# Moving the block for over-full experts from the middle of the expert layer to its end

## The chip, the cores and the metric

The kernel runs on one core of one Trainium2 chip. The metric is device time in microseconds (us), taken as the median of several executions. A profile of one further execution gives the trace from which all rows below are read. The engines are called PE (matrix multiply; PEld is its weight load), ACT (activations), DVE (vector), POOL and SP; SP does no arithmetic here and issues nearly all DMA transfers.

## The reference, cut to what matters

Two layers, each with a mixer and then a mixture of experts. A token goes to two of 32 experts; each expert is a gated pair of products and a third product. What the change touches is the second half of a layer:

```python
def hier_moe(u, w_grp, b_grp, w_rt, b_rt, w1, w3, w2):
    ...
    eid = (g_idx * EXP_PER_GROUP + e_idx).reshape(TK)      # T = 512 tokens, TOP_K = 2
    ...
    def expert_block(args):
        xr, e = args
        return (jax.nn.silu(xr @ w1[e]) * (xr @ w3[e])) @ w2[e]
    ...

for layer in range(2):
    ...
    h = h + gt1 * m
    u = rms_norm(h, norm2[layer]) * (1.0 + sc2) + sh2
    h = h + gt2 * hier_moe(u, ...)
return rms_norm(h, final_norm)
```

The sum over experts is added to h, so the order of the experts is free as far as the sum goes. What follows the layer (the next layer's norm, or the final norm) needs the sum of squares of each row of the finished h.

## The kernel before, in words

h stays in SBUF as four tiles of 128 tokens by 1024 (`self.h(t)`, the tile `w` in the trace). The expert layer (`moe`, L1387) first routes: `posm` holds each token's place within its expert, `wcat` its weight. The 32 experts are then taken in 16 pairs, with 64 slots (`CAP`) for each expert. For two pairs at a time, PE multiplies the normalised tokens `hhi`/`hlo` with a one-hot matrix `Dm` (L1427) and so gathers the inputs `XTm`. For each pair PE computes the two products with w1 and w3 (L1506), ACT and DVE form `gg`, PE transposes it (L1536) and multiplies with w2 (L1560), and POOL, ACT and DVE form `yh`/`yl`. The step that adds a pair's result to h (`add`, L1567: PE L1574, DVE L1583) is put off: it is handed on as `before` and runs inside the next pair's step, in two halves, so that PE has work while DVE and ACT make `gg` and `hT`. Near the start of each pair POOL writes the small tile `sel` (L1515).

The weights of a pair are 12 MB, 12 transfers of 1 MB. `need` (L1365) issues them in a fixed order into some 15 buffers; a transfer waits until PE has read the buffer's last content. So SP's queue is a long row of transfers, each of which waits for PE.

An expert can get more than 64 tokens. For these, `overflow` (L1679) is a loop on the device: each turn takes 128 further tokens of such an expert, gathers them, fetches that expert's weights again and adds to h. The number of turns `nblk` is computed by `blocks` (L1666) and loaded into a register by every engine (L1686); the loop starts at L1688. The loop stands between the eighth and the ninth pair. Ahead of it the eighth pair's `add` is run out, so nothing is handed on across it. With the inputs used here no expert has more than 64 tokens in either layer: `nblk` is zero, and no instruction of the loop's body stands in the trace. What every engine does there is load the register, branch past the body, and wait at the loop's end: SP until all transfers that it has issued have landed, each engine until all engines and all transfer queues have reached their counts.

In the last pair, ACT squares each piece of h right after its last addition (L1587), with the sum going to `hss`; the squares themselves are not needed and are written over `hhi`. After layer 0 `restart` (L1912) takes the square root (`h_rstd`, L387), scales h into `hn`, and PE transposes that (L532); after layer 1 `finish` (L1825) multiplies the lower half of h with `fn`, the final norm's weights, on POOL (L1832), scales it on ACT (L1835), makes the upper half on DVE (L1836), and SP and ACT send the four tiles out (L1837).

Between Silu and Sqrt the compiled program holds a table load on ACT, an instruction of its own. `warm` (L1548) is a Sqrt of one element in the last pair, whose only use is that this load happens early.

Of the kernel before, what the change touches and what calls it, by code (L numbers as in the profile page):

```python
# [7 lines left out]
F32 = mybir.dt.float32  # L8
# [3 lines left out]
AF = mybir.ActivationFunctionType  # L12
OP = mybir.AluOpType
# [4 lines left out]
P = 128  # L18
D = 1024
# [3 lines left out]
EPS = 1e-6  # L23
# [1 line left out]
DE = 512  # L25
CAP = 64
BIG = 4096
OVER = 8
NPOOL = 3
PRI = 80  # L30
PIN = 12
# [11 lines left out]
def spread(x, h):  # L43

    return [x[:, c + j:c + 256:2] for c in (512 * h, 512 * h + 256) for j in range(2)]


def row_bcast(ap, n, parts=P):
    return bass.AP(tensor=ap.tensor, offset=ap.offset, ap=[[0, parts], [1, n]])
# [41 lines left out]
class Build:  # L91
# [1295 lines left out]
    def moe(self, es):  # L1387
        tc, nc, a, M = self.tc, self.nc, self.a, self.M
        l = M.l
        pool = M.pool  # L1390
        A, B = self.mod[l, 4], self.mod[l, 3]
        total = self.n_ext + 8
        M.more = self.pool(es, "more%d" % l, 2, side="right")
        first = ExitStack()
        M.first = self.pool(first, "first%d" % l, 2, side="right")
        posm = pool.tile([P, NT, NE], F32, name="posm")
        wcat = pool.tile([P, NT, 2, NE], F32R, name="wcat")
        self.need(total + 2)
        gate = self.gate_rows(l, 5)
        self.warm(WARM)  # L1400
        self.dump("lg%d" % l, M.lg)
        blocks = self.route(M.rt, M.lg, posm, wcat)
        self.dump("posm%d" % l, posm)
        M.rt_es.close()
        wk = self.pool(es, "mw%d" % l, 2)

        def onehot(e0):

            Dm = wk.tile([P, NT, 4, CAP], F32R, name="Dm", tag="Dm", bufs=1)
            with tc.high_priority(0 if e0 else PRI):  # L1410
                for t in range(NT):
                    nc.vector.tensor_tensor(Dm[:, t], posm[:, t, e0:e0 + 4, None].to_broadcast([P, 4, CAP]),
                                            self.slot_row[:, None, :].to_broadcast([P, 4, CAP]), op=OP.is_equal)
            return Dm

        inputs = lambda: wk.tile([P, KD, 4 * CAP], F32, name="XTm", tag="XTm", bufs=1)

        def dispatch(e0, Dm, XT):

            if not e0:  # L1420
                M.low()
            def blocks(ks):
                for k in ks:
                    p = self.ps([P, 4 * CAP])
                    for t in range(NT):
                        for i, src in enumerate((M.hhi, M.hlo)):
                            nc.tensor.matmul(p, spread(src[:, t], k // 4)[k % 4], Dm[:, t].rearrange("p e s -> p (e s)"),  # L1427
                                             start=t + i == 0, stop=t == NT - 1 and i == 1)
                    if k % 2:
                        nc.scalar.activation(XT[:, k], p, AF.Identity, scale=A[:, k:k + 1], bias=B[:, k:k + 1])  # L1430
                    else:
                        nc.vector.tensor_scalar(XT[:, k], p, A[:, k:k + 1], B[:, k:k + 1], op0=OP.mult, op1=OP.add)
            return Dm, XT, blocks


        XT = inputs()
        cur = dispatch(0, onehot(0), XT)

        self.need(total + 4)
        blocks = blocks()  # L1440
        before = Dnew = None
        for pr in range(NE // 2):
            if pr == OVER:
                for hb in range(2):
                    before(hb)
                before = None
                self.overflow(l, wk, wy, *blocks, posm, wcat, A, B, gate)

            self.need(12 * (pr + 1) + (total - 1 if pr == OVER - 1 else total))
            Dm, XT, make = cur  # L1450
            q = pr % 2
            tiles = [M.tiles.pop(12 * pr + i) for i in range(12)]
            p13 = self.ps(), self.ps()
            last = pr == NE // 2 - 1
            X = XT[:, :, q * P:(q + 1) * P]
            if not pr:

                for ks in range(4), range(4, KD):
                    make(ks)
                    for j in range(2):  # L1460
                        self.expert_in(p13, X, tiles, j, ks)
            else:
                self.expert_in(p13, X, tiles, 0, range(KD))
                if last:
                    for i in range(2):
                        before(i)
                    before = None
                self.expert_in(p13, X, tiles, 1, range(KD))
            if not pr:
                first.close()  # L1470
                wy = self.pool(es, "my%d" % l, 1, side="right")
                posT = wy.tile([NE, T], F32R, name="posT")
                p = self.ps([NE, T])
                for t in range(NT):
                    nc.tensor.transpose(p[:, t * P:(t + 1) * P], posm[:, t], self.ident)
                nc.vector.tensor_copy(posT, p)

            new = q and not last

            def early():  # L1480
                nonlocal Dnew
                if new:
                    Dnew = onehot(2 * pr + 2)

            def late():
                nonlocal cur
                if new:
                    cur = dispatch(2 * pr + 2, Dnew, inputs())
                    cur[2](range(KD))
            if last and l:  # L1490

                M.fn = wk.tile([P, D], F32, name="fn", tag="XTm", bufs=1)
                nc.sync.dma_start(M.fn, row_bcast(self.a["final_norm"], D))
            before = self.expert_pair(l, pr, *p13, tiles,
                                      lambda t: Dm[:, t].rearrange("p e s -> p (e s)")[:, q * P:(q + 1) * P],
                                      wk, wy, posT, wcat, gate, before, early, late)
        for i in range(len(M.cols)):
            before(i)

    def expert_in(self, ps, X, tiles, j, ks):  # L1500

# [6 lines left out]
    def expert_pair(self, l, pr, p1, p3, tiles, Dp, wk, wy, posT, wcat, gate, before, early, late):  # L1508


        nc, a, M = self.nc, self.a, self.M
        pin = self.tc.keep_in_program_order
        ea, last = 2 * pr, pr == NE // 2 - 1
# [37 lines left out]
        for c in cols:  # L1551
            py = self.ps([P, c.stop - c.start])
            hb = c.start // DE
# [13 lines left out]
        def add(n):  # L1567
            s = cols[n]
            if not (pr or n):
                self.new_h()  # L1570
            for t in range(NT):
                p = self.ps([P, s.stop - s.start])
                for i, y in enumerate((yh, yl)):
                    mm = nc.tensor.matmul(p, dt[:, t * P:(t + 1) * P], y[:, s], start=i == 0, stop=i == 1)  # L1574
                    if not last:
                        pin(mm)
                h = self.h(t)[:, s]
                part = lambda x, o: nc.vector.scalar_tensor_tensor(h, x[:, t, s].bitcast(F32), M.sd[:, t:t + 1], o,
                                                                   op0=OP.mult, op1=OP.add)
                if not pr:  # L1580
                    part(M.hhi, p)
                else:
                    nc.vector.tensor_add(h, h, p)  # L1583
                    if t == pr - 1:
                        part(M.hlo, h)
                if last:
                    nc.scalar.activation(M.hhi[:, t, s], h, AF.Square, accum_out=self.hss[:, n, t:t + 1])  # L1587
            if last and n == 1:
                nc.vector.tensor_add(self.hss[:, 0], self.hss[:, 0], self.hss[:, 1])
                nc.vector.tensor_scalar(self.hss[:, 0], self.hss[:, 0], 1.0 / D, EPS, op0=OP.mult, op1=OP.add)  # L1590
# [88 lines left out]
    def overflow(self, l, wk, wy, nblk, ends, over, posm, wcat, A, B, gate):  # L1679

        tc, nc, a, M = self.tc, self.nc, self.a, self.M
# [6 lines left out]
        with tc.For_i(0, n, 1):  # L1688
# [81 lines left out]
            for s in hs:  # L1770
                y32 = wy.tile([P, DE], F32, name="oy", tag="y32")
                nc.vector.scalar_tensor_tensor(y32, py[s.start // 512], wsl, gate[:, s], op0=OP.mult, op1=OP.mult)
                nc.scalar.activation(yh[:, s], y32, AF.Copy)
                nc.vector.tensor_sub(yl[:, s], y32, yh[:, s].bitcast(F32))
                for t in range(NT):
                    p = self.ps()
                    for i, y in enumerate((yh, yl)):
                        nc.tensor.matmul(p, DT[:, t], y[:, s], start=i == 0, stop=i == 1)
                    nc.vector.tensor_add(self.h(t)[:, s], self.h(t)[:, s], p)
            nc.vector.tensor_scalar(it, it, 1.0, None, op0=OP.add)  # L1780


# [178 lines left out]
```

## Time and profile before

| | |
|---|---|
| time, median of 3 executions | 1754.81 us (1753.83 to 1755.5) |
| the profiled execution: time | 1752.5 us |
| the profiled execution: span from first to last instruction | 1750.8 us |
| granted PE clock, mean over the span (1 is 2.4 GHz, 0.5 is 1.2 GHz) | 0.973 |
| PE busy | 1653.0 us (94%) |
| DVE, ACT, POOL busy | 804.0, 514.8, 394.8 us |
| HBM read | 492.21 MB |

Busy times are sums over stages with different limits, so they bound nothing by themselves. A stage is read from the windows of that stage; a stall is read from the idle time that the profile puts before an instruction, with the one that ended it.

### The profile page before, as it was taken

How to read it: one execution, taken by the hardware profiler on the slowest of the kernel's cores; microseconds unless marked ns; L12 is line 12 of the kernel's file. 1: busy time of each engine (PE TensorE's matmuls, PEld its weight loads, DVE VectorE, ACT ScalarE, POOL GpSimd, SP SyncE). 2: the span in 40 equal slices, each digit the busy share in tenths (PEclk: the TensorE clock that was granted, in tenths of full speed). 3: DMA queues.
4: the chain of work that ended last, by engine and by line, in shares of the span. 5: the costliest groups of instructions: out<-in, count | busy, mean ns of one | idle time of the engine just before them, and what ended most of it. 6: DMA issues, size and time to landing. Idle time of an engine off the chain costs nothing. (4 is left out here: it accounts for less than half of the span.)

```text
span 1750.8 us, 23258 instructions
## 1 busy us (share of the span) xinstructions
PE 1653.0 (94%) x9036; PEld 992.8 (57%) x9036; DVE 804.0 (46%) x1793; ACT 514.8 (29%) x1025; POOL 394.8 (23%) x350
## 2 busy tenths in 40 slices
PE   6999999899999899998989989899899999899997
PEld 3666767544555445454667667678544555455453
DVE  3345653432424224235787787855433334224234
ACT  4745333310110111014636475364310110111013
POOL 2443532210101001002534343353210011001001
PEclk9999999999999999999989999999999999999998
DMA  8655655689999899995233432237699999899994
GB/s 299 222 187 174 219 179 204 258 344 379 413 412 412 346 410 414 412 411 165 65 126 123 134 108 93 77 112 274 237 368 380 414 411 413 345 410 413 412 411 144
DMA packets 156052, 495.90 MB, mean 283 GB/s; under 512 B 16216, under 2 KB 43156, under 8 KB 140576
## 3 DMA queue, kind: packets, MB, share of 16 engines
q1 hardware_dynamic: 155488, 493.23, 73.2%
q8 instruction: 74, 1.21, 0.3%
q10 hardware_dynamic: 448, 1.11, 0.2%
q14 instruction: 42, 0.34, 0.1%
HBM read 492.21 MB, written 2.10 MB: 282 GB/s over the span
## 5 line engine op out<-in xcount | busy, mean ns | idle before, releaser
L1506 PE MATMUL ps<-w,XTm 128*64 128x512 f32 x2048 | 450.8, 597 | 11.5 <-SPq L1688 10.9
L1506 PEld LDWEIGHTS ps<-w,XTm 128*64 128x64 f32 x2048 | 155.8, 138 | 289.5 <-issue 281.1
L397 POOL TENSOR_TENSOR wlo<-w,whi 128x512 fp32r<-128x512 f32 x136 | 180.6, 1332 | 278.7 <-ACT whi L396 257.3
L1560 PE MATMUL ps<-w,hT 128*64 128x512 f32 (+1 forms) x1056 | 232.3, 590 | 1.6 <-ACT hT L1538 1.6
L1529 DVE TENSOR_TENSOR gg<-gg,ps 128x512 f32<-128x512 f32 x32 | 22.0, 688 | 395.6 <-PE ps L1506 395.6
L403 PE MATMUL ps<-w,whi 128*128 128x512 f32 x384 | 164.4, 429 | 0.1
L404 PE MATMUL ps<-w,whi 128*128 128x512 f32 x384 | 155.9, 406 | 2.2 <-POOL w L527 1.5
L1560 PEld LDWEIGHTS ps<-w,hT 128*64 128x64 f32 x1056 | 80.3, 138 | 134.2 <-issue 120.2
L405 PE MATMUL ps<-w,wlo 128*128 128x512 f32 x384 | 155.2, 405 | 0.0
L1583 DVE TENSOR_TENSOR w<-w,ps 128x512 f32<-128x512 f32 (+1 forms) x248 | 149.4, 662 | 8.5 <-PE ps L1574 7.2
L1515 POOL CAST sel<-ident 32x128 fp32r<-32x128 f32 x32 | 9.0, 281 | 617.0 <-PE ps L1543 499.9
L1564 POOL TENSOR_TENSOR yl<-y,yh 128x512 fp32r<-128x512 f32 x60 | 76.6, 1276 | 242.7 <-ACT yh L1563 242.7
L396 ACT ACTIVATE whi<-w 128x512 fp32r<-128x512 f32 x136 | 84.5, 626 | 145.6 <-PE ps L404 77.6
L1427 PE MATMUL ps<-Dm,hhi 128*128 128x256 f32 x512 | 125.8, 288 | 0.1
L1563 ACT ACTIVATE yh<-y 128x512 fp32r<-128x512 f32 (+1 forms) x66 | 40.8, 618 | 287.3 <-DVE y L1562 286.7
L1427 PE MATMUL ps<-Dm,hlo 128*128 128x256 f32 x512 | 123.4, 283 | 0.0
L1562 DVE SCALAR_TENSOR_TENSOR y<-ps,wsl,gate 128x512 f32<-128x512 f32 (+1 forms) x66 | 48.5, 734 | 147.4 <-PE ps L1560 72.4
L1427 PEld LDWEIGHTS ps<-Dm,hhi 128*128 128x128 f32 x512 | 101.1, 198 | 13.7 <-issue 13.5
L1574 PE MATMUL ps<-yh,dt 128*128 128x512 f32 (+1 forms) x264 | 105.6, 405 | 0.0
L1538 ACT ACTIVATE hT<-ps 128x512 f32<-128x512 f32 x32 | 19.1, 598 | 281.8 <-PE ps L1536 263.5
L1427 PEld LDWEIGHTS ps<-Dm,hlo 128*128 128x128 f32 x512 | 101.2, 198 | 0.0
L1574 PE MATMUL ps<-yl,dt 128*128 128x512 f32 (+1 forms) x264 | 100.8, 387 | 0.2 <-DVE yl L1564 0.2
(519 smaller groups left out, 2423.3 us busy)
## 6 DMA issues: line engine op xcount, KB each, us to landing
w<-in_moe_w_dram SPq DMA_DIRECT2D x380, 1024.0 KB, 12.6
w<-in_w_ada_dram SPq DMA_DIRECT2D x40, 1024.0 KB, 5.5
w<-in_w_in_c_dram SPq DMA_DIRECT2D x16, 1024.0 KB, 6.1
w<-in_w_in_ab_dram SPq DMA_DIRECT2D x10, 1024.0 KB
wst<-in_w_ada_dram SPq DMA_DIRECT2D x8, 1024.0 KB, 12.3
w<-in_w_out_ab_dram SPq DMA_DIRECT2D x4, 1024.0 KB, 4.8
w<-in_moe_w_dram SPq DMA_DIRECT2D x8, 512.0 KB, 10.4
w<-in_w_out_c_dram SPq DMA_DIRECT2D x4, 1024.0 KB, 4.8
```

The lines of the kernel that those rows point to most:

```text
L396: nc.scalar.activation(hi, src, AF.Copy)
L397: nc.gpsimd.tensor_sub(lo, src, hi.bitcast(F32))
L403: mm(p, lhs[0], rhs[0], start=start, stop=False)
L404: mm(p, lhs[0], rhs[1], start=False, stop=False)
L405: mm(p, lhs[1], rhs[0], start=False, stop=stop)
L1427: nc.tensor.matmul(p, spread(src[:, t], k // 4)[k % 4], Dm[:, t].rearrange("p e s -> p (e s)"), start=t + i == 0, stop=t == NT - 1 and i == 1)
L1506: self.nc.tensor.matmul(ps[j][half[e]], X[:, k, half[e]], w, start=k == 0, stop=k == KD - 1)
L1560: nc.tensor.matmul(py[half[e]], hT[:, k, half[e]], w, start=k == 0, stop=k == 3)
L1562: nc.vector.scalar_tensor_tensor(y32, py, wsl, gate[:, c], op0=OP.mult, op1=OP.mult)
L1564: (nc.vector if last else nc.gpsimd).tensor_sub(yl[:, c], y32, yh[:, c].bitcast(F32))
L1574: mm = nc.tensor.matmul(p, dt[:, t * P:(t + 1) * P], y[:, s], start=i == 0, stop=i == 1)
L1583: nc.vector.tensor_add(h, h, p)
```

## The change

The call of `overflow` moves from ahead of the ninth pair to behind the last one, in both layers. Its code is the same but for two lines at its end, which the new place asks for: since h can still change there, each turn squares h again. As the loop's body still needs `hhi`, the last pair's squares go to a scratch area `M.squares` of 1024 columns, half of the tile `fn`, that all four token tiles share.

```diff
         for pr in range(NE // 2):
-            if pr == OVER:
-                for hb in range(2):
-                    before(hb)
-                before = None
-                self.overflow(l, wk, wy, *blocks, posm, wcat, A, B, gate)
-
-            self.need(12 * (pr + 1) + (total - 1 if pr == OVER - 1 else total))
+            self.need(12 * (pr + 1) + total)
...
-            if last and l:
-
-                M.fn = wk.tile([P, D], F32, name="fn", tag="XTm", bufs=1)
-                nc.sync.dma_start(M.fn, row_bcast(self.a["final_norm"], D))
+            if last:
+
+                fn = wk.tile([P, 2, D], F32, name="fn", tag="XTm", bufs=1)
+                M.fn, M.squares = fn[:, 0], fn[:, 1]
+                if l:
+                    nc.sync.dma_start(M.fn, row_bcast(self.a["final_norm"], D))
...
         for i in range(len(M.cols)):
             before(i)
+        self.overflow(l, wk, wy, *blocks, posm, wcat, A, B, gate)
...
-                    nc.scalar.activation(M.hhi[:, t, s], h, AF.Square, accum_out=self.hss[:, n, t:t + 1])
+                    nc.scalar.activation(M.squares[:, s], h, AF.Square, accum_out=self.hss[:, n, t:t + 1])
...
                     nc.vector.tensor_add(self.h(t)[:, s], self.h(t)[:, s], p)
+                    nc.scalar.activation(M.squares[:, s], self.h(t)[:, s], AF.Square,
+                                         accum_out=self.hss[:, 1 + s.start // 512, t:t + 1])
+            nc.vector.tensor_scalar(self.hss[:, 0], self.hss[:, 1], 1.0 / D, EPS, op0=OP.mult, op1=OP.add)
             nc.vector.tensor_scalar(it, it, 1.0, None, op0=OP.add)
```

On SP, in the expert layer of layer 0, the loop stood between the weight transfers of before (`nblk` is the register load at the loop's entry; the body begins with the load of `ei`):

```order
L132 DMA w<-in_moe_w_dram 128x2048 x4
L132 DMA w<-in_moe_w_dram 128x2x1024 x2
L1686 TENSOR_LOAD nblk
L1688 COMPARE_AND_BRANCH
L1688 UNCONDITIONAL_BRANCH x2
L1956 BRANCH_PREFETCH_HINT
L1733 TENSOR_LOAD ei
```

In the changed kernel SP reaches it behind all weight transfers of the layer and behind the first transfers of the next layer's mixer; here is its end, with what follows:

```order
L1249 DMA wr<-in_moe_w_grp_dram 128x2x4
L1682 TENSOR_LOAD nblk
...
L1684 REGISTER_ALU
L1684 COMPARE_AND_BRANCH
L1684 UNCONDITIONAL_BRANCH
L1249 DMA wr<-in_moe_w_grp_dram 128x2x4
L1249 DMA wr<-in_moe_w_rt_dram 128x2x32 x2
L1252 DMA br<-in_moe_b_grp_dram 128x4
L1253 DMA br<-in_moe_b_rt_dram 128x32
L134 DMA w<-in_w_ada_dram 128x4x512
```

So one transfer of 1 MB (`in_w_ada`) and five small ones, which were issued while the last pair ran, now follow the loop. On ACT, the end of layer 0 reads before as follows (the squares write `hhi`, `hr` is the square root, `whi` a rounded copy of the next mixer's weights):

```order
L1587 ACTIVATE hhi,hsq<-w 128x512
L1587 ACTIVATE hhi,hsq<-w 128x256 x6
L396 ACTIVATE whi<-w 128x512
L1587 ACTIVATE hhi,hsq<-w 128x256 x2
L387 ACTIVATE hr<-hsq 128x1 x3
L1919 ACTIVATE hn<-w,hr 128x512 x3
L387 ACTIVATE hr<-hsq 128x1
L396 ACTIVATE whi<-w 128x512
L1919 ACTIVATE hn<-w,hr 128x512
```

and in the changed kernel as follows:

```order
L1583 ACTIVATE fn,hsq<-w 128x256 x8
L1682 TENSOR_LOAD nblk
L1684 COMPARE_AND_BRANCH
...
L1684 UNCONDITIONAL_BRANCH
L386 ACT_TABLE_LOAD
L386 ACTIVATE hr<-hsq 128x1 x4
L1918 ACTIVATE hn<-w,hr 128x512 x4
L395 ACTIVATE whi<-w 128x512 x2
```

The loop now stands between the squares and the roots. Since its body holds a Silu, a table load stands behind it, whether or not the body runs. The first copies `whi` stand behind `hn`. On POOL, at the end of layer 1, the four products `out` stood right behind the last `yl` (which is written for the last pair but one), free to start as soon as h is final:

```order
L1564 TENSOR_TENSOR yl<-y_13258,yh 128x512
L1832 TENSOR_TENSOR out<-w,fn 128x512 x4
```

In the changed kernel the loop stands ahead of them, as it does on each engine; in layer 0 POOL's first steps for the next mixer are moved behind it in the same way:

```order
L1560 TENSOR_TENSOR yl<-y_13024,yh 128x512
L1682 TENSOR_LOAD nblk
L1684 COMPARE_AND_BRANCH
L1684 UNCONDITIONAL_BRANCH x2
L1955 BRANCH_PREFETCH_HINT
L1684 REGISTER_ALU
L1684 COMPARE_AND_BRANCH
L1684 UNCONDITIONAL_BRANCH
L1831 TENSOR_TENSOR out<-w,fn 128x512 x4
```

## Rows read from the trace of the kernel before

**Rows 1.** The page's first part: busy time and share, PE's line.

```profile
PE 1653.0 (94%) x9036; PEld 992.8 (57%) x9036; DVE 804.0 (46%) x1793; ACT 514.8 (29%) x1025; POOL 394.8 (23%) x350
```

**Rows 2.** Windows of layer 0: stretch, its length, busy per engine, clock, DMA share and GB/s.

```profile
core 0: us, PE busy (x) PEld busy (x) DVE busy (x) ACT busy (x) POOL busy (x), PEclk, DMA share, GB/s
499.00:559.00 60.00, 60.00 (x307) 31.76 (x306) 20.76 (x39) 7.18 (x12) 5.68 (x6) 1.00 1.02 413
...
578.00:583.00 5.00, 0.00 (x0) 0.00 (x0) 1.51 (x3) 0.00 (x0) 0.00 (x0) 0.77 0.58 229
583.00:587.00 4.00, 3.94 (x10) 1.24 (x12) 0.00 (x0) 0.00 (x0) 0.00 (x0) 0.50 0.59 200
...
818.00:824.50 6.50, 2.88 (x19) 2.39 (x18) 6.14 (x17) 5.69 (x25) 3.52 (x5) 0.89 0.00 1
```

**Rows 3.** Timeline of POOL: the tile `sel`, around the middle of either layer.

```profile
559.33 0.28 POOL L1515 CAST sel<-ident 32x128 fp32r<-32x128 f32 x1 [14.34 <-PE ps L1543]
...
627.71 0.28 POOL L1515 CAST sel<-ident 32x128 fp32r<-32x128 f32 x1 [16.18 <-PE ps L1543]
...
687.71 0.28 POOL L1515 CAST sel<-ident 32x128 fp32r<-32x128 f32 x1 [16.20 <-PE ps L1543]
...
1478.33 0.28 POOL L1515 CAST sel<-ident 32x128 fp32r<-32x128 f32 x1 [14.34 <-PE ps L1543]
...
1546.48 0.28 POOL L1515 CAST sel<-ident 32x128 fp32r<-32x128 f32 x1 [16.18 <-PE ps L1543]
```

**Rows 4.** Timeline of PE: after the loop (either layer), after layer 0, an `in_w_ada` reader.

```profile
583.06 1.97 PE L1506 MATMUL ps<-w,XTm 128*64 128x512 f32 x4 [5.28 <-SPq L1688]
...
826.24 3.82 PE L532 MATMUL ps<-ident,hn 128*128 128x128 f32 x16 [5.35 <-ACT hn L1919]
...
870.70 1.06 PE L259 MATMUL ps<-w,cond 128*32 128x512 f32 x8
...
1502.40 1.98 PE L1506 MATMUL ps<-w,XTm 128*64 128x512 f32 x4 [5.64 <-SPq L1688]
```

**Rows 5.** Sequencer events of L1688 by engine: duration min/median/max ns, first and last start.

```profile
L1688 SPq EVENT_SEMAPHORE  x17: 17/17/28, 567.4 to 583.1; - x17
...
L1688 DVEq EVENT_SEMAPHORE  x3: 21/50/50, 579.5 to 580.3; - x3
...
L1688 ACTq EVENT_SEMAPHORE  x8: 38/38/38, 1501.3 to 1501.9; - x8
```

**Rows 6.** Timeline of ACT at the end of layer 0.

```profile
808.74 1.28 ACT L1548 ACT_TABLE_LOAD   x1
810.03 0.20 ACT L1548 ACTIVATE warm<-one 128x1 f32<-128x1 f32 x1
...
820.10 0.40 ACT L1587 ACTIVATE hhi<-w 128x256 fp32r<-128x256 f32 x1
820.41 0.19 ACT L1587 ACTIVATION_READ_ACCUMULATOR hhi<-w 128x1 f32 x1
820.50 0.40 ACT L1587 ACTIVATE hhi<-w 128x256 fp32r<-128x256 f32 x1
...
823.81 0.65 ACT L387 ACTIVATE hr<-hsq 128x1 f32<-128x1 f32 x3
825.47 1.95 ACT L1919 ACTIVATE hn<-w,hr 128x512 f32<-128x512 f32 x3 [1.01 <-DVE hr L388]
```

**Rows 7.** Timeline of SP, the issues at the end of layer 0.

```profile
805.11 1.26 SPq L1250 DMA_DIRECT2D wr<-in_moe_w_grp_dram  x2
...
812.45 0.38 SPq L135 DMA_DIRECT2D w<-in_w_ada_dram  x1
```

**Rows 8.** Timelines of ACT, POOL and DVE at the end of layer 1.

```profile
1742.26 0.19 ACT L1587 ACTIVATION_READ_ACCUMULATOR hhi<-w 128x1 f32 x1
...
1745.82 0.36 ACTq L1837 DMA_DIRECT2D out_dram<-out  x1
...
1734.81 5.32 POOL L1832 TENSOR_TENSOR out<-w,fn 128x512 f32<-128x512 f32 x4 [22.46 <-DVE w L1583]
...
1742.28 0.75 DVE L1836 SCALAR_TENSOR_TENSOR out<-w,hr,fn 128x512 f32<-128x512 f32 x1
```

More of the change, by code (lines that the diff above doesn't have):

```diff
@@ L27 @@
 BIG = 4096
-OVER = 8
 NPOOL = 3
```

## The prediction

> **What bounds the kernel now.** I read the page first, then windows of the expert stage, the timelines around the loop, and last the two layer ends. The page has PE busy for 94% of the span [rows 1]. In the expert stage that is no average: in 60 us of steady pairs PE is busy for all 60.00 us, at full clock, while the transfers run at a share of 1.02 and 413 GB/s [rows 2]. So any time that PE stands there is lost, and nothing makes it up later. The pace can be counted at `sel`, which POOL writes once per pair: two pairs of the steady stage take 60.0 us (627.71 to 687.71), but the two pairs across the loop take 68.38 us in layer 0 (559.33 to 627.71) and 68.15 us in layer 1 (1478.33 to 1546.48) [rows 3]. The loop, which does nothing here, costs 8.4 and 8.15 us, 16.5 us together.
>
> Three parts of it can be seen. PE stands for 5.28 and 5.64 us, ended by SP's L1688 [rows 4]. Then its first matmuls run at a granted clock of 0.50, the level of 1.2 GHz: 4.0 us of work at half speed, some 2 us lost [rows 2]. The rest, about 1 us, goes at the start of the ninth pair, which has no handed-on `add` to fill its gaps. Why PE stands that long: SP spends 567.4 to 583.1 in the loop's waits [rows 5], and transfers it had issued were still moving at 229 GB/s in the standstill [rows 2]. The wait is for weights in flight, not for arithmetic.
>
> **What is removed.** Without the loop the eighth and ninth pairs are a pair of pairs like any other, and DVE, ACT and POOL get the order that they have at the other pairs. I take the whole of it: -16.5 us. The bounds: if only the standing time came back, -5.28 - 5.64 = -10.9 us; more than the 16.5 us that are over the pace can't come back.
>
> **What is added, in general.** At the layer's end the loop's wait is no longer for a busy stream. Its last small transfers ahead of the loop are issued at about 806 in layer 0 [rows 7], some 18 us before the squares end, with a DMA share of 0.00 from 818 on [rows 2]. What is left is the passage itself. DVE's three events bound it: its own count at 579.5, the next two by 580.3, so about 0.7 us to get past the branch; eight waits take 0.6 us on ACT (1501.3 to 1501.9) [rows 5]; and one more branch, 0.1 to 0.5 us (PE restarts at 1502.40 [rows 4]). I take 1.4 us for the engine that comes last, ACT. Bounds: 1.0 us, if ACT's branch is as short as its waits, and 8.4 us, the whole price in the middle.
>
> **The scratch area.** The squares now share one output, so ACT waits for itself: of the last eight, six (three of four in each column range) wait for the square before. Now a square starts 0.40 us after the last one, before that one's read of the sum has ended (820.50 against 820.41 + 0.19) [rows 6]. Waiting for the end makes it 0.50 us and a signal; I take 0.53, so +0.8 us in each layer, with bounds of 0 and 1.2.
>
> **End of layer 0.** Eight squares from 820.10 at 0.40 us, the last ending 0.49 after its start, are done at 823.4; with 0.8 for the scratch area, at 824.2. The passage brings 825.6. A table load takes 1.28 us: 826.9. Four roots follow at 0.19 us (three took 0.65, their ends overlapping): `hn` starts at 827.6, against 825.47 [rows 6]. PE followed 0.77 us behind `hn` (826.24 [rows 4]), so it starts at 828.4 instead of 826.24: **+2.1 us**. Before, PE idled 5.35 us there [rows 4] already, so the wait only grows.
>
> At nothing I cost three things. POOL's and DVE's preparations for the next mixer (POOL was busy for 3.52 us between 818 and 824.5 [rows 2], the last squares' own time) now come after the loop; ACT's table load, roots and scaling, 825 to 828.4, hide them, and without that cover they would cost up to those 3.5 us. The `in_w_ada` transfer moves from 812.45 [rows 7] to about 828, and its reader, the L259 matmul, is at 870.70 [rows 4]; only a delay of over 40 us would show. The register loads run while the last square is still at work. Bounds of this end: +0.9 us (passage 1.0, no self-wait, the roots as now) and +8.4.
>
> **End of layer 1.** The last square ends at 1742.45 [rows 8], 1742.26 without the root that stood among them; with the self-waits less the slack that DVE's additions leave, 1742.9. POOL has only to see ACT's count and starts its four products at 1743.2. They take 5.32 us [rows 8], which lay beside the last additions before: 1748.5, and ACT's scaling of the last tile with its issue needs 0.8 more: 1749.3. ACT's own way is as long: 1742.9 + 1.4 + 1.28 = 1745.6, a root 0.28 and its reciprocal, then four DVE products from 1746 at 0.75 us each [rows 8] and the reciprocals between them: 1749.2. The last output was issued at 1745.82 [rows 8], so **+3.5 us**. Bounds: +2.5 (passage 1.0, no self-wait) and +8.4. What is late next is the last output transfer, and nothing is behind it.
>
> **Sum.** -16.5 + 2.1 + 3.5 = -10.9 us. Made against the profiled execution that is 1752.5 - 10.9 = 1741.6 us, with a span of 1739.9. That execution lies 2.3 us under the median of 1754.8, so the median should be **1743.9, say 1744 us**. The bounds, all at their low end: -16.5 + 3.4 = -13.1; all at their high end: -10.9 + 16.8 = +5.9.
>
> **A rule against a row.** ACT's load of 808.74 ends at 810.02 and the next activation starts at 810.03; nothing stands before or after it [rows 6]. The Trainium skill, "ScalarE: Activation LUTs", section "What ACT_TABLE_LOAD costs", has the same 1283 ns, but adds a drain of about 1380 ns to every switch, 2.66 us in all. By that each end would be some 1.4 us later and the sum -8.1 us, an estimate from that page. The row shows no such drain at this load, so I go by the row.
>
> **The rivals.**
> A slower switch: behind the loop ACT pays for its table load twice, since something empties first. Priced by the row, a second 1.28 us at each end: -8.3 us, 1746.5. Against it is the row just read; for it, that this load stands behind a branch, which no row shows. The rule from the Trainium skill's "ScalarE: Activation LUTs" that is weighed above leads here.
> Only the standing time comes back: half speed and the thin start of the ninth pair are made up by something else, and the removal brings 10.9: -5.3 us, 1749.5. Against it, the pace of 60.0 us on either side.
> The loop costs at the ends what it cost in the middle, 8.4 and 8.15 us: no change, 1755. For it, the same waits stand there; against it, no stream is in flight.
> Slower: each engine, after it has jumped over the body, stands until its next instructions are fetched, and where all five have nothing else to do that is laid bare. Its place is the branch behind the loop at both ends. It takes the gain away from 5.5 us per end on, over the forecast; at 8.4 us per end, the whole price of the middle once more, the sum is -10.9 + 16.8 = +5.9: 1761. Against it: in the middle PE starts at 583.06 [rows 4], when SP's last wait in the loop (583.1) [rows 5] has hardly begun, with the transfer queues just emptied as they are at the ends, so no long fetch stands behind the branch there.
>
> **How the numbers follow.** A measurement of this kernel can tell about 0.2%, 3.5 us, from no change. My forecast (-13 to -7 us) gets 0.68, the slower switch or a passage of that price (-8 to -3.5, where it isn't in the forecast) 0.13, only the standing time 0.06, the full price at the ends 0.08, slower 0.05. So faster 0.87, same 0.08, slower 0.05. The range of eight in ten leaves out the last two cases and the low end's tail: 1741 to 1750; the likeliest case alone is 1741 to 1748.
>
> **What would show it.** In the changed profile the `sel` rows should be 60.0 us apart per two pairs throughout, with no PE wait on the loop's line and no window at 0.50 in the middle. At the end of layer 0 PE's idle time ahead of L531 should be near 7.5 us in place of 5.35, with a table load of 1.28 us in ACT's row behind the loop. At the end of layer 1 POOL's four `out` should begin after the last square and end about 1 us before the last output's issue. The prediction is wrong if the pace stays at 68 us across the ninth pair, if SP's waits in the loop last on a landing at the layer's end, or if PE stands for more than 13 us there.

## The result, and the profile after

The changed kernel takes 1746.17 us (median of 5 executions, 1745.99 to 1747.66) against 1755.5 us (1753.83 to 1758.77) for the kernel before, run in turns with it: a ratio of 0.9944, 95% interval 0.9933 to 0.9955, or 9.3 us less. The forecast was 10.9 us less, 1744, with a range of 1741 to 1750. The profiled execution took 1746.73 us, with a span of 1745.0 us and a mean granted clock of 0.973.

First the middle, where the loop stood. The timeline of POOL in the changed kernel, the tile `sel` around the place where the loop stood, in layer 0 and in layer 1:

```profile
560.75 0.28 POOL L1511 CAST sel<-ident 32x128 fp32r<-32x128 f32 x1 [14.34 <-PE ps L1539]
...
621.14 0.28 POOL L1511 CAST sel<-ident 32x128 fp32r<-32x128 f32 x1 [14.65 <-PE ps L1539]
...
680.92 0.28 POOL L1511 CAST sel<-ident 32x128 fp32r<-32x128 f32 x1 [14.34 <-PE ps L1539]
...
1475.38 0.28 POOL L1511 CAST sel<-ident 32x128 fp32r<-32x128 f32 x1 [14.34 <-PE ps L1539]
...
1535.48 0.28 POOL L1511 CAST sel<-ident 32x128 fp32r<-32x128 f32 x1 [14.36 <-PE ps L1539]
```

The two pairs across the loop's old place now take 60.39 us in layer 0 and 60.10 in layer 1, where they took 68.38 and 68.15; the next two of layer 0 take 59.78, where they took 60.00 [rows 3]. The windows of the same kernel (stretch, length, busy per engine, clock, DMA share, GB/s) show that nothing stands there any more; the last two are the end of layer 0:

```profile
core 0: us, PE busy (x) PEld busy (x) DVE busy (x) ACT busy (x) POOL busy (x), PEclk, DMA share, GB/s
499.00:559.00 60.00, 60.00 (x307) 31.69 (x306) 20.77 (x39) 7.18 (x12) 5.66 (x6) 1.00 1.02 412
...
578.00:583.00 5.00, 5.00 (x26) 1.72 (x24) 0.00 (x0) 0.29 (x1) 0.00 (x0) 1.00 1.02 406
...
816.00:822.00 6.00, 0.20 (x1) 0.21 (x2) 3.93 (x10) 4.44 (x13) 2.24 (x4) 0.62 0.11 14
822.00:828.00 6.00, 6.00 (x27) 5.01 (x27) 4.48 (x11) 5.84 (x10) 3.90 (x4) 0.53 0.55 177
```

PE is busy for 5.00 of 5.00 us at full clock where it stood for the same 5 us in the kernel before, while transfers moved at 229 GB/s [rows 2]. At the end of layer 0 PE now stands until 821.80, and the 6 us that follow run at a mean granted clock of 0.53.

Then the ends. To compare kernels whose starts differ by a few us, I count from the last `sel` of a layer: 775.11 and 1689.74 in the changed kernel, and, from the timeline of POOL in the kernel before:

```profile
781.89 0.28 POOL L1515 CAST sel<-ident 32x128 fp32r<-32x128 f32 x1 [22.38 <-PE ps L1543]
...
1700.66 0.28 POOL L1515 CAST sel<-ident 32x128 fp32r<-32x128 f32 x1 [22.38 <-PE ps L1543]
```

ACT in the changed kernel, its timeline at the end of layer 0 and at that of layer 1:

```profile
816.45 0.42 ACT L1583 ACTIVATE fn<-w 128x256 f32<-128x256 f32 x1
...
816.99 0.42 ACT L1583 ACTIVATE fn<-w 128x256 f32<-128x256 f32 x1
817.32 0.19 ACT L1583 ACTIVATION_READ_ACCUMULATOR fn<-w 128x1 f32 x1
818.99 1.28 ACT L386 ACT_TABLE_LOAD   x1 [1.48 <-issue]
820.28 0.85 ACT L386 ACTIVATE hr<-hsq 128x1 f32<-128x1 f32 x4
821.04 2.59 ACT L1918 ACTIVATE hn<-w,hr 128x512 f32<-128x512 f32 x4
...
1731.94 0.19 ACT L1583 ACTIVATION_READ_ACCUMULATOR fn<-w 128x1 f32 x1
1733.42 1.28 ACT L386 ACT_TABLE_LOAD   x1 [1.29 <-issue]
1734.71 0.67 ACT L386 ACTIVATE hr<-hsq 128x1 f32<-128x1 f32 x3
...
1740.01 0.37 ACTq L1836 DMA_DIRECT2D out_dram<-out  x1
```

The squares start 0.54 us apart (816.45, 816.99), not 0.40 [rows 6]. From the end of the last read of a sum to the table load is 1.48 us at this end and 1.29 us at that of layer 1: the passage. The load takes 1.28 us, and the first root follows 0.01 us behind it. The timeline of PE:

```profile
821.80 3.88 PE L531 MATMUL ps<-ident,hn 128*128 128x128 f32 x16 [7.69 <-DVE hn L1919]
...
835.41 1.09 PE L540 MATMUL ps<-w,wba 128*32 128x512 f32 x8
```

PE restarts 821.80 - 775.11 = 46.69 us after the last `sel`, against 826.24 - 781.89 = 44.35 [rows 4]: +2.34 us. The next mixer's L540, which PE reaches in both kernels behind the first products of that mixer, comes 60.30 us after the last `sel`, against 57.84 before. At the end of layer 1 POOL and DVE in the changed kernel read (two timelines):

```profile
1732.47 5.37 POOL L1831 TENSOR_TENSOR out<-w,fn 128x512 f32<-128x512 f32 x4 [31.05 <-ACTq L1684]
...
1735.24 1.48 DVE L1835 SCALAR_TENSOR_TENSOR out<-w,hr,fn 128x512 f32<-128x512 f32 x1
1736.65 0.21 DVE L387 RECIPROCAL hr<-hr 128x1 f32<-128x1 f32 x2
1736.83 2.22 DVE L1835 SCALAR_TENSOR_TENSOR out<-w,hr,fn 128x512 f32<-128x512 f32 x2
1738.98 0.15 DVE L387 RECIPROCAL hr<-hr 128x1 f32<-128x1 f32 x1
1739.17 0.75 DVE L1835 SCALAR_TENSOR_TENSOR out<-w,hr,fn 128x512 f32<-128x512 f32 x1
```

DVE's products that lie beside POOL's (until 1737.84) take about twice 0.75 us, and the last, alone, takes 0.75. The last output is issued 1740.01 - 1689.74 = 50.27 us after the last `sel`, against 1745.82 - 1700.66 = 45.16 [rows 8]: +5.1 us.

### The profile page after: what moved, and what is told of

Read it like the earlier page. It is cut to its first block, busy times and chain, and to the rows that moved or that the text cites. A ratio compares the mean times of both kernels' runs of the same rounds, so it can differ in the third digit from the quotient of the medians.

```text
span 1745.0 us, 23263 instructions
## 1 busy us (share of the span) xinstructions
PE 1651.2 (95%) x9036; PEld 1003.2 (57%) x9036; DVE 806.4 (46%) x1793; ACT 518.9 (30%) x1027; POOL 394.8 (23%) x350
## 5 line engine op out<-in xcount | busy, mean ns | idle before, releaser
L1502 PEld LDWEIGHTS ps<-w,XTm 128*64 128x64 f32 x2048 | 161.7, 137 | 267.6 <-issue 260.7
```

The lines of the kernel that those rows point to most:

```text
L1502: self.nc.tensor.matmul(ps[j][half[e]], X[:, k, half[e]], w, start=k == 0, stop=k == KD - 1)
```

## The experiments

All were timed in turns with the kernel before. From each one's trace five stretches were read as above: in each layer from the sixth pair's `sel` to the sixteenth's (middle), from the last `sel` of layer 0 to L531 and to L540, and from that of layer 1 to the last output's issue. (Line numbers of the copies differ by a few.)

| kernel | median us | ratio to before (95%) | middle 0 | middle 1 | to L531 | to L540 | to last issue |
|---|---|---|---|---|---|---|---|
| before | 1755.2 to 1755.8 | 1 | 308.6 | 308.5 | 44.35 | 57.84 | 45.16 |
| changed | 1746.17 | 0.9944 (0.9933 to 0.9955) | 300.4 | 300.5 | 46.69 | 60.30 | 50.27 |
| no loop | 1740.54 | 0.9918 (0.9902 to 0.9934) | 300.4 | 300.5 | 45.06 | 58.90 | 45.83 |
| end in layer 0 only | 1749.72 | 0.9971 (0.9958 to 0.9983) | 300.4 | 308.8 | 46.67 | 60.28 | 45.17 |
| end in layer 1 only | 1752.51 | 0.9981 (0.9968 to 0.9993) | 308.5 | 300.5 | 44.33 | 57.82 | 50.27 |
| middle, twice | 1761.77 | 1.0038 (1.0025 to 1.0052) | 311.1 | 314.4 | 44.33 | 57.82 | 45.15 |
| end, twice | 1749.58 | 0.9965 (0.9953 to 0.9977) | 300.4 | 300.5 | 48.40 | 61.68 | 51.79 |
| squares apart | 1742.05 | 0.9928 (0.9913 to 0.9943) | 300.4 | 300.5 | 45.68 | 58.88 | 49.35 |
| Sqrt in the body | 1745.37 | 0.9942 (0.9927 to 0.9957) | 300.4 | 300.5 | 46.57 | 60.29 | 50.04 |
| lower products on DVE | 1745.21 | 0.9940 (0.9926 to 0.9955) | 300.4 | 300.5 | 46.69 | 60.41 | 48.74 |
| these three together | 1740.76 | 0.9916 (0.9901 to 0.9931) | 300.4 | 300.5 | 45.59 | 58.87 | 48.19 |
| columns behind `hn` | 1745.66 | 0.9946 (0.9932 to 0.9961) | 300.4 | 300.5 | 45.21 | 61.14 | 50.07 |
| four edits | 1744.36 | 0.9938 (0.9925 to 0.9951) | 300.4 | 300.5 | 44.23 | 60.16 | 46.72 |
| four edits, columns later | 1738.50 | 0.9903 (0.9886 to 0.9919) | 300.4 | 300.5 | 44.24 | 58.55 | 46.73 |

The stretches are the same to 0.15 us wherever a kernel leaves them alone, but for 0.4 us in a middle that holds the loop. The rest of the program (start, mixers) differs by some us from one execution to the next, and so do the places at which the granted clock dips (from 200 to 225 us its mean is 0.93 in the kernel before and 0.86 in the changed one, with the same code); so a single us is told by the stretches and not by the medians.

**The loop taken away.**

```diff
         for i in range(len(M.cols)):
             before(i)
-        self.overflow(l, wk, wy, *blocks, posm, wcat, A, B, gate)
```

> The changed kernel with the call of the loop left out in both layers (no turn of it runs with these inputs); the shared scratch area stays. It measures what the loop still costs at the two ends. My theory: at each end the loop costs ACT's passage of 1.45 us and the table load of 1.28 us behind it (both read from the changed kernel's ACT rows), and at the end of layer 1 another 1.5 us for DVE products that run beside POOL's; the shared scratch costs some 0.8 us per end and stays. So 5.5 to 7 us below the changed kernel, about 1739.5 to 1741, which is 14.5 to 16 us below the kernel before; PE's idle time ahead of L531 some 5.9 us instead of 7.7. Rival, that the passage is nearly free and the ends' loss comes from the squares and the clock: no more than 2 us below the changed kernel. Rival, that the loop still costs at the ends a good part of its price in the middle: 10 us or more below it.

Measured: 5.6 us below the changed kernel, at the low end of what I expected. At the end of layer 1 the loop costs 50.27 - 45.83 = 4.4 us, as my theory had it (1.45 + 1.28 + 1.5). At that of layer 0 it costs 1.63 us at L531 and 1.40 at L540, where the theory had 1.45 + 1.28 = 2.73. The missing 1.1 us stand in the rows of the kernel without the loop (timelines of DVE and of ACT):

```profile
820.21 0.12 DVE L387 RECIPROCAL hr<-hr 128x1 f32<-128x1 f32 x1
...
820.36 1.49 ACT L1917 ACTIVATE hn<-w,hr 128x512 f32<-128x512 f32 x2 [1.18 <-DVE hr L387]
```

DVE's copies and its transpose for the next mixer lie ahead of that reciprocal, and ACT waits 1.18 us for it. In the kernel before, ACT waited 1.01 us there in the same way [rows 6]. So about 1 us of ACT's longer way through the loop only fills a wait that was there already. The 0.7 us (45.06 and 45.83 against 44.35 and 45.16) that are left without the loop are put down to the shared scratch area, the only other edit at the ends.

**One layer at a time.**

```diff
+            if l != END and pr == OVER:
...
+                self.overflow(l, wk, wy, *blocks, posm, wcat, A, B, gate)
...
+        if l == END:
+            self.overflow(l, wk, wy, *blocks, posm, wcat, A, B, gate)
```

> The loop moved to the end in layer 0 only; layer 1 has it in the middle, with squares written as before. My theory: the two layers add up, and each gives its 8.2 or 8.0 us in the middle and pays its own end. Layer 0: -8.2 + 2.3 = -5.9 us against the kernel before, about 1749.5; the two expert stages then show a pace of 60.0 us for two pairs across the ninth pair in layer 0 and 68 in layer 1. Rival, that one layer carries the whole gain of 9 us: under -8 or over -2 us here.

> The loop moved to the end in layer 1 only; layer 0 has it in the middle. My theory: -8.0 + 5.1 = -2.9 us against the kernel before, about 1752.5, with POOL's and DVE's products at the end of layer 1 colliding as in the changed kernel. The sum of this run's and the other layer's differences should be the whole change's -9.3 us within 1.5 us. Rival, that the ends cost the same in both layers (3.5 each): -4.5 us in each.

Measured: 6.1 and 3.3 us below the kernel before (1755.83 in this group), 9.4 together, where the whole change gave 9.3. Each layer's middle gives back 8 us, and each pays its own end; the layers do not touch each other.

**The loop twice in a row, in the middle and at the ends.**

```diff
                 self.overflow(l, wk, wy, *blocks, posm, wcat, A, B, gate)
+                self.overflow(l, wk, wy, *blocks, posm, wcat, A, B, gate)
```

> The kernel before with the loop called twice in a row at its place in the middle, in both layers. When the second call is reached, nothing that SP has issued is still in flight. My theory, that the wait in the middle is for weights in flight and that the passage itself is short: the second call adds only the passage, 1.5 to 2.5 us per layer with what SP needs to come past it, so 3 to 5 us in all, 1758.5 to 1760.5. Rival, that the loop itself costs the 8 us wherever it stands (fetching instructions behind the branch, clearing its queues): +13 to +17 us, about 1770. Rival, that a second loop is wholly hidden by the first one's wait: within 1 us of the kernel before.

> The changed kernel with the loop called twice in a row at each end. Called twice in the middle, the second pass cost 2.4 us in layer 0 and 5.9 in layer 1, where PE's branch past the body lasted 3.35 us instead of 0.3 to 0.7. This asks what a pass costs where nothing is in flight. My theory: a pass is 2.0 to 2.5 us on ACT's way (register load, branches, eight waits), so 4 to 5 us in all, 1750 to 1751.5. Rival, that a branch past the body can stand until instructions arrive, and that this falls on PE or ACT here too: 3 us more at an end, with one branch of over 3 us in the rows. Rival, that the second pass hides behind the first: under 1.5 us in all.

Measured in the middle: +5.9 us by the medians, between my theory and the first rival; by the stretches 8.4. The two profiled executions differ by 8.7 us (1761.2 and 1752.5); that of the kernel before lies 3.3 us under its median of this group, and where the medians' other 2.5 us are, no row says. The second pass, with nothing in flight, adds 2.4 us in layer 0, as expected, but 5.9 in layer 1. The group of the loop's line in that kernel (engine, operation, count; ns min/median/max; first and last start) shows what stood; the same group in the second pass alone (1505 to 1511) shows which engine was late; and the DMA queues from 1505.2 to 1508.8 show what moved meanwhile:

```profile
L1689 ACTq COMPARE_BRANCH  x12: 32/36/49, 575.3 to 1506.4; - x12
L1689 PEldq COMPARE_BRANCH  x12: 70/178/3348, 576.0 to 1509.6; - x12
```

```profile
L1689 PEldq EVENT_SEMAPHORE  x9: 51/51/51, 1505.2 to 1509.5; - x9
L1689 ACTq EVENT_SEMAPHORE  x8: 38/38/38, 1505.5 to 1506.4; - x8
```

```profile
q14 instruction: 3, 0.02, 2.4%
q8 instruction: 1, 0.02, 1.6%
```

One of PE's branches past the body (PEldq is the sequencer that issues PE's weight loads) lasts 3.35 us, while on the other engines none is over 0.07, and PE's last wait in the loop starts 3.1 us behind ACT's. So the branch accounts for most of the 3.5 us by which layer 1's second pass is dearer than layer 0's. Why the branch lasts is not shown. Queues that the profile calls instruction queues move a few packets meanwhile, but they do so in stretches without a long branch too (from 578 to 584 in the kernel before: two on q14, one on q8); that the branch waited for one of them is a guess. The Trainium skill, "Runtime: NRT & Kernel Launch", section "Instruction fetch mechanics", says that a taken branch to a target outside the loaded pages stalls until the page is fetched, and gives no time for it. No run here shows whether this branch is such a case.

Measured at the ends: 3.4 us, less than the 4 to 5 expected: 1.7 us more to L531, 1.5 to the last issue. No branch there is over 0.4 us. So a pass costs 1.5 to 1.7 us on ACT's way where nothing is in flight, and most of the 8 us of the middle came from the wait for the stream.

The changed kernel has such a long branch too, at the end of layer 1 (the same view of its loop's line there):

```profile
L1684 PEldq COMPARE_BRANCH  x3: 70/183/3282, 1728.5 to 1733.1; - x3
L1684 ACTq COMPARE_BRANCH  x3: 33/33/39, 1732.0 to 1733.3; - x3
```

It costs nothing that shows: PE is at the loop over 3 us ahead of ACT, its last branch (1733.1) is still ahead of ACT's (1733.3), and ACT's passage there is 1.29 us, no longer than at the end of layer 0.

**Squares with a part of their own.**

```diff
-                M.fn, M.squares = fn[:, 0], fn[:, 1]
+                M.fn, M.squares = fn[:, 0], fn[:, 1].bitcast(BF).rearrange("p (t d) -> p t d", t=NT)
...
-                    nc.scalar.activation(M.squares[:, s], h, AF.Square, accum_out=self.hss[:, n, t:t + 1])
+                    nc.scalar.activation(M.squares[:, t, s.start % 512:s.start % 512 + s.stop - s.start], h, AF.Square, accum_out=self.hss[:, n, t:t + 1])
```

> The changed kernel, with the last pair's squares written in bf16 to an area that has a part of its own for each token tile, so that a square need no longer wait for the one before it. My theory: the pitch of the last squares returns from 0.54 us to 0.40 and each end gains 0.6 to 1 us: 1.2 to 2 us below the changed kernel, some 1744.5. Rival, that the pitch is set by the additions that feed the squares: same time within 0.5 us and a pitch of 0.54.

Measured: 4.1 us below the changed kernel by the medians, more than the 1.2 to 2 expected. The stretches show 1.4 (L540) and 0.9 of it; the rest lies in other stretches, mostly the mixer between the layers, and I don't count it. ACT's timeline at the end of layer 0 has the pitch of 0.40 again:

```profile
815.46 0.40 ACT L1583 ACTIVATE fn<-w 128x256 bf16<-128x256 f32 x1
...
815.86 0.40 ACT L1583 ACTIVATE fn<-w 128x256 bf16<-128x256 f32 x1
```

So the pitch was ACT's wait for itself, not the additions'. (The edit also makes the output bf16; that this is not the cause is seen in the kernel before, where outputs of four bytes with a part of their own had the pitch of 0.40 too [rows 6].)

**No table load behind the loop.** The new line is the last but one of the loop's body.

```diff
+            nc.scalar.activation(wsl, wsl, AF.Sqrt)
             nc.vector.tensor_scalar(it, it, 1.0, None, op0=OP.add)
```

> The changed kernel with a Sqrt of one element at the end of the loop's body (which does not run), so that the compiled program needs no table load behind the loop. My theory: the load costs its own 1.28 us at each end and nothing besides, so 2.6 us below the changed kernel at most, and, since at the end of layer 1 POOL's products run beside ACT's way and DVE's, 1.3 to 2.6 us: about 1744. Rival, that a switch also empties something for as long again: 2.7 us at each end, 4 to 5.3 us, about 1741.5. Rival, that another wait takes its place: under 0.7 us.

Measured: as the last rival has it, another wait takes the load's place. To L531 the edit gains 0.12 us, to the last issue 0.23, though the load is gone. At the end of layer 0 the reason stands in DVE's timeline of that kernel:

```profile
818.53 2.45 DVE L920 COPY Yt<-ident 32x256 f32<-32x256 f32 x2
821.01 0.22 DVE L387 RECIPROCAL hr<-hr 128x1 f32<-128x1 f32 x2
```

The roots came 1.3 us earlier, but their reciprocals stood behind DVE's first two copies for the next mixer. In the changed kernel these two end just as early, and the first of them lasts 2.15 us by itself. POOL's memsets lie beside it (the changed kernel's timelines of DVE, over a longer and a shorter stretch, and of POOL):

```profile
818.24 2.45 DVE L920 COPY Yt<-ident 32x256 f32<-32x256 f32 x2
820.72 0.23 DVE L387 RECIPROCAL hr<-hr 128x1 f32<-128x1 f32 x2
...
818.24 2.15 DVE L920 COPY Yt<-ident 32x256 f32<-32x256 f32 x1
...
818.25 0.95 POOL L925 MEMSET X<- 128x1024 f32 x1
819.14 0.95 POOL L926 MEMSET XT<- 128x1024 f32 x1
820.02 0.23 POOL L932 MEMSET gd<- 128x160 f32 x1
```

At the end of layer 1 the load's 1.28 us went to DVE's products, which then lay wholly beside POOL's: 1.55 us, then 3.23 for two. ACT's rows without the load also say what a switch costs: from the last read to the first root are 1.50 and 1.30 us, against 1.48 and 1.29 from the last read to the load in the changed kernel. So the load costs its own 1.28 us on ACT's way and nothing besides.

**The lower products on DVE; and the three together.**

```diff
-            nc.gpsimd.tensor_mul(out[t][:, lo], self.h(t)[:, lo], fn[:, lo])
+            nc.vector.tensor_mul(out[t][:, lo], self.h(t)[:, lo], fn[:, lo])
```

> The changed kernel with the four products of the lower half in the last stage made by DVE instead of POOL. DVE stands idle between the loop and the first reciprocal there for some 2.5 us. My theory: DVE's first two upper products took 1.48 and 1.56 us instead of 0.75 because POOL's products ran beside them; without these all eight stand near 0.75 or below, and the end comes 1 to 1.5 us earlier: about 1745, which is at the edge of what can be told. Shown by the products' own durations in any case. Rival, that the first products are slow for another reason (a first use, the reciprocal's result): they stay at 1.5 us and the end comes later by DVE's added work.

> The changed kernel with the three edits together: squares with a part of their own for each token tile, the Sqrt in the loop's body in place of a table load behind it, the lower products on DVE. My theory: the three terms are on the same path one behind the other, so they add up: 0.7 + 1.3 us at the end of layer 0 and 0.7 + 1.3 + 1.2 at that of layer 1, some 5 us below the changed kernel, about 1741, and 14 below the kernel before. Rival, that POOL's or DVE's products become the bound at the end of layer 1 once ACT's way is short: 3 to 3.5 us, about 1743.

DVE's timeline of the first at the end of layer 1:

```profile
1733.37 2.50 DVE L1831 TENSOR_TENSOR out<-w,fn 128x512 f32<-128x512 f32 x4 [1.88 <-ACTq L1684]
...
1736.27 2.06 DVE L1835 SCALAR_TENSOR_TENSOR out<-w,hr,fn 128x512 f32<-128x512 f32 x3
...
1738.43 0.75 DVE L1835 SCALAR_TENSOR_TENSOR out<-w,hr,fn 128x512 f32<-128x512 f32 x1
```

With POOL silent the upper products are back at 0.69 to 0.75 us, and the end is 1.53 us shorter: the first products were slow because of POOL's. The three together take 1740.76, 5.4 us below the changed kernel, the median that was expected. But the stretches show only 1.43 (L540) and 2.08 us of it, 3.5 together, which is the rival's figure, and no run says where the other 1.9 us are. Not all three terms add up: the Sqrt in the body gains next to nothing at the end of layer 0, and at that of layer 1 DVE's lower products are the next wait.

**DVE's copies out of the way.** Two tries. The first sets them behind the layer end's last `hn`. It was run with the Sqrt alone ("columns behind `hn`"), and with the squares apart and the lower products made ahead of the loop as well, and again in each turn of its body ("four edits"):

```diff
-            first_columns()
+            with tc.issue_after(self.last_hn.ins):
+                first_columns()
...
+        low = None
+        if l:
+            low = M.low = self.slot(M.loaded).tile([P, NT, DE], F32, name="w", tag="w")
+            for t in range(NT):
+                nc.gpsimd.tensor_mul(low[:, t], self.h(t)[:, :DE], M.fn[:, :DE])
+        self.overflow(l, wk, wy, *blocks, posm, wcat, A, B, gate, low)
...
```

> The changed kernel with the Sqrt in the loop's body, as in the run before of that name, and with DVE's four copies for the next mixer (Yt) set behind its last hn of the same layer end. With the Sqrt alone PE's idle time ahead of L531 stayed at 7.6 us, though the table load was gone. My theory: DVE's first copy of Yt, 0.28 us alone, lasted 2.15 us beside POOL's two memsets and held the reciprocals, so the 1.28 us came to nothing there. With the copies behind hn the reciprocals follow the roots at once: PE restarts some 1.35 us earlier, 45.2 us after the last sel instead of 46.6, with an idle time of 6.3 us, and the whole is near 1744. Rival, that something else holds the reciprocals or PE there (a transfer, a clock level): the restart stays at 46.5 us after the last sel.

> The changed kernel with what the runs point to: squares with a part of their own for each token tile, the Sqrt in the loop's body, DVE's copies of Yt behind hn, and the lower products of the last stage made by POOL ahead of the loop, beside the last additions, and again in each turn of its body. My theory: PE restarts some 44.2 us after the last sel of layer 0 (46.7 in the changed kernel, 44.35 before); at the end of layer 1 neither POOL's products nor DVE's lie behind the loop, and the last output is issued some 46.3 us after the last sel (50.3 changed, 45.2 before). Together 6.5 us below the changed kernel, 1738 to 1740, and below the three edits together by 1 to 3 us. Rival, that POOL's products now hold up the loop itself or DVE's additions: the end of layer 1 stays at 48 us.

The stretches came near what was expected, 45.21 and 44.23 us to L531 and 46.72 to the last issue, and yet the four edits took 1744.36, 3.6 us more than the three and above the expected 1738 to 1740. One reason shows: the gain was gone at L540 (61.14 and 60.16, against 58.87 with the three). But the end of layer 1 came 1.5 us earlier, so the stretches don't make up the 3.6 us; where the rest is stays open. In the first kernel's timelines of DVE and of PE:

```profile
821.95 3.27 DVE L920 COPY Yt<-ident 32x256 f32<-32x256 f32 x4
...
826.45 1.37 PE L531 MATMUL ps<-ident,hn 128*128 128x128 f32 x8 [0.63 <-DVE uf L525]
```

Now the copies lay beside POOL's next products, and PE waited for DVE's `uf`, behind them. So the second try sets them behind `copied`, the copy to `bap`, ahead of which DVE waits for PE anyway:

```diff
-            first_columns()
+            with tc.issue_after(copied.ins):
+                first_columns()
```

> As the run with squares of their own, the Sqrt in the body, Yt behind hn and the lower products ahead of the loop, but with DVE's four copies of Yt behind its bap copy, where DVE waited 3.5 us for PE, instead of right behind hn. In that run PE restarted early, as forecast (44.23 us after the last sel), and yet L540 came 60.16 us after the last sel, against 60.30 in the changed kernel and 58.87 with the three edits together: the copies, 3.27 us beside POOL's products there, stood ahead of DVE's uf, for which PE waited next. My theory: out of the way of both, L540 comes 57.5 us after the last sel, as before the change (57.84), the end of layer 1 stays at 46.7, and the whole is near 1738, 1736.5 to 1740. Rival, that the next step is bound by something else as well (POOL's products, the clock after PE's wait): L540 stays at 58.9 or later and the whole at 1740 or above.

Measured: 1738.50 us, the fastest here, 17 us below the kernel before. In DVE's timeline the four copies take what they take alone:

```profile
837.92 1.17 DVE L920 COPY Yt<-ident 32x256 f32<-32x256 f32 x4
```

L540 came at 58.55, a us later than the forecast 57.5 and just ahead of the rival's 58.9: after PE had stood for 5.24 us, its first 4 us ran at a granted clock of 0.50, the level of 1.2 GHz, and it still waited twice for ACT. The stretches show 1.6 us of the 5.9 us by which the median lies under the first try's; so the place of the copies is shown to give 1.6 us and not more.

## Why the prediction was right, point by point

**What is removed** (-16.5): right. The middles became 8.19 and 7.97 us shorter, 16.2 us. That standing time, half speed and the thin start of the ninth pair all come back is read from the pace; what each of them is worth by itself no run shows. That the wait was for weights in flight is shown by the second pass, which has none in flight and costs 1.5 to 2.4 us where PE's long branch is not laid bare.

**End of layer 0** (+2.1): right, +2.34. The passage was 1.48 us against 1.4, the scratch area cost 0.7 to 1.0 us at L531 against 0.8, the table load its 1.28 us with no drain. The step that costed POOL's and DVE's preparations at nothing, covered by ACT's table load, roots and scaling, held with nothing to spare. The roots start at 820.28, and the first reciprocal at 820.72, right behind DVE's second copy; with the load taken away, DVE's copies held the end for nearly the same time. That DVE's way came out no longer than ACT's was luck: I had costed POOL's own busy time there, and not what POOL does to DVE's copies.

**End of layer 1** (+3.5): the way was right, a size was off: +5.1 us. The mis-sized term is "four DVE products from 1746 at 0.75 us each". They took 1.48 us, 2.22 for two and 0.75, with the reciprocals 4.7 us from first start to last end, where I had 3.2. The step that failed is the price: the 0.75 of [rows 8] was measured with POOL at rest; I moved POOL's four products beside DVE's and kept it. With the lower products on DVE the 1.5 us come back. The Trainium skill, "SBUF — State Buffer", section "Who interferes with whom", says that a DVE instruction with two SBUF inputs contends with a POOL instruction that reads SBUF, and that a DVE copy can, under conditions, contend with POOL as well. The trace agrees, 0.75 to 1.48 us for the one and 0.28 to 2.15 for the other; I hadn't drawn on it.

**The sum** (-10.9): measured -9.3, and by the stretches -16.2 + 2.3 + 5.1 = -8.8. Of the 2.1 us between forecast and stretches, 1.6 are that term; 0.3 are the middle and 0.2 the end of layer 0.

**The rivals.** A slower switch: the root starts 0.01 us behind the table load, so no second 1.28 us; the drain of about 1380 ns in the Trainium skill's "ScalarE: Activation LUTs", section "What ACT_TABLE_LOAD costs", does not show in this row either, nor ahead of the load: the gap there is the same with the load and without it. Only the standing time: the pace of 60 us rules it out. The full price at the ends: a pass there costs 1.5 to 1.7 us, and the whole ends grew by 2.3 and 5.1. Slower by a branch that stands: its argument against, that no long fetch stands behind the branch, was wrong as a rule. Such a branch exists, 3.28 us in the changed kernel, on one engine of the five and under cover. With the loop twice in a row in the middle it was laid bare once, in layer 1.

**What would show it**: each item came as written (two pairs within 0.4 us of 60.0, PE idle for 7.69 us ahead of L531) but the last, since POOL's four `out` ended 2.2 us before the last issue instead of 1, DVE being that much later.

## What to carry to other kernels

A device loop that runs no turn still waited here until everything in flight had landed, so it belongs where no stream is: it cost 8 us per layer inside the weight stream, and 1.5 to 1.7 us for a pass without one. What comes behind it is laid bare, so price each moved instruction beside its new neighbours and not by a row from where it was alone, DVE beside POOL above all. And when a term is taken off such an end, read on to the next place that PE waits for: a copy moved out of one wait went straight into the next.

## What the runs showed of the hardware

A DVE copy of 32x256 float32 takes 0.28 us alone (four take 1.17, above) and 2.15 us beside POOL's memsets: it ended only when all three of these, one behind the other, had ended, and not after the first. The kernel before already had such a row, 1.31 us beside a POOL product of 1.27 us (timeline of DVE):

```profile
823.30 1.31 DVE L921 COPY Yt<-ident 32x256 f32<-32x256 f32 x1
```

The longest of PE's branches at the loop lasted about 0.3 to 0.8 us in most passes and 3.3 to 3.7 us in others: at the end of layer 1 in nine of the ten kernels that have the loop there (not in the one that has it twice), and in the middle of layer 1 in its second pass. On the other engines no branch was over 0.07 us. Why it is this place and this engine stays open.
